# Two conditioning vectors of layer 1: summed along rows by DVE beside the gate projection, in place of matmuls in the attention

## The chip, the cores and the metric

The kernel runs on one core of a Trainium2 chip. The time is device microseconds of one execution of the whole program. Engines: PE (TensorE, matmuls), DVE (VectorE), ACT (ScalarE), POOL (GpSimd) and SP, which here only issues DMAs. Each engine works through its own queue in order; semaphores order them against each other.

## What is computed

One step of a two-layer trunk on 512 latent tokens and 128 context tokens of width 1024. Layer 0 mixes tokens by gated attention, layer 1 by a gated linear recurrence. The change touches only the conditioning: each layer derives a shift, a scale and a gate from two vectors (`c` for latent tokens, `c_ctx` for context tokens).

```python
def _adaln(cond, w, b):
    mod = jax.nn.silu(cond.astype(jnp.float32)) @ w.astype(jnp.float32) + b.astype(jnp.float32)
    mod = mod.astype(cond.dtype)
    return jnp.split(mod, 3, axis=-1)

for i in range(DEPTH):
    sh_p, sc_p, g_p = _adaln(c_ctx, ada_w[i], ada_b[i])
    sh_s, sc_s, g_s = _adaln(c, ada_w[i], ada_b[i])
    hp = xp * (1.0 + sc_p) + sh_p
    hs = xs * (1.0 + sc_s) + sh_s
    ...
```

So per layer there is a product of a 2 x 1024 matrix with a 1024 x 3072 matrix (12 MB of weights). Layer 0's shift and scale are needed before anything else; layer 0's gate at its output projection; layer 1's shift and scale after layer 0; layer 1's gate at the end.

## The kernel before

Tokens lie in five tiles of 128 (`TT`), features in eight (`KT`). Float32 products are made of three matmuls of split operands (high and low part), so each weight piece of 128 x 1024 is loaded (`raw`), cast by ACT to its high part (`whi`, L232) and reduced to its low part by DVE (`wlo`, L233).

The first half of the program (up to the output projection of layer 0) is put in order by a scheduler that works on a simulated timeline; DMAs and some other instructions wrapped in `pin` keep their program order. The stages there are:

- lead-in, to about 55 us: layer 0's shift and scale (`ada_feat`, from `ada_m`), the modulated input `hhi`/`hlo`, keys and values (`acc`);
- query chunk 0 (`pmm`) and then the gate projection (`gps`, 16 steps of 24 matmuls over the weight chunks 6 to 9). In its steps the list `later` splits the queries of chunk 0 (`q_job`: `qn`, `u`, `r`, then `qs`) and the keys (`k_split`, `klo`), and PE turns them (`qps`, `kps`). The norm of the queries takes a power on POOL (`rq`) behind DVE's `rs_t`;
- attention (`att_gen`): scores `sc`, row maximum `nm` on DVE (L936), exponential `p` on ACT (L941), its scaling on POOL (L947), transposes `pt`, products `pot`. Two units of scores run ahead of the products. Beside it a list `side` is woven in at a fixed ratio: the query chunks 1, 2, 3 (`q_gen`, `qmm`), and then the loading and splitting of the output weights.

What the change touches is `ada_gen`. The vectors `ada_s` are four blocks of 1024 x 1024: 0 is layer 0's gate, 1 and 2 are layer 1's shift and scale, 3 is layer 1's gate. Each is eight pieces (`raw`, 512 KB); `ada_mms` (L276) multiplies a piece with the Silu of the vectors, on 32 columns of the array per quarter, and DVE adds the result into `acc` (L327). Block c − 1 runs in the filler of query chunk c, block 3 behind the last of them:

```python
    def q_next(c):
        Xs[c] = xq[c % 2].tile([P, 4, NT], F32R, tag="X", name=f"X{c}")
        yield from q_gen(c, Xs[c], ada_gen((c - 1,)))
    ...
    side.items.append(("a", ada_gen((3,)), lambda: back_of[0] == 3))
```

All weight pieces come through one ring of three buffers (`rawp`) in the order of the list `order`, at most two ahead (`RAW_AHEAD`), issued by SP.

Of the kernel before, what the change touches and what calls it, by code (L numbers as in the profile page):

```python
# [11 lines left out]
F32 = mybir.dt.float32  # L12
# [6 lines left out]
P = 128  # L19
# [28 lines left out]
D_ST = 3.0  # L48
D_OUT = 5.5
SLIP = 1.0  # L50


def view(t, off, dims):
# [78 lines left out]
def hybrid_step(ctx: ExitStack, tc: tile.TileContext, a: dict, o: dict):  # L132
# [62 lines left out]
    def pump():  # L195
        while order:
            start = order[0] in FIRST
            if len(ahead) >= (RAW_START if start else RAW_AHEAD):
                break
            src = order.popleft()  # L200
            if src[0] == "x":
                c = slice(src[1] * CW, (src[1] + 1) * CW)
                pin(nc.sync.dma_start(xt[:, :TS, c], a["xs"][:, c].rearrange("(t p) d -> p t d", p=P)))
                pin(nc.sync.dma_start(xt[:, TS, c], a["xp"][:, c]))
                continue
            if src[0] == "rope":
                rope_loads()
                continue
            raw = (raw0 if start else rawp).tile([P, 1024], F32, tag="raw", name="raw")
            if src[0] == "kvh":  # L210
                pin(nc.sync.dma_start(raw[:, :512], piece(src)))
            else:
                (pass_on if src[0][:3] == "rec" else pin)(nc.sync.dma_start(raw, piece(src)))
            ahead.append((src, raw))

    def piece(src):
        name, c, i = src
        if name == "kvh":
            return a["attn_kv"][0][:, i * 512:(i + 1) * 512]
        if name == "ada_s":  # L220
            return a[name][c][i * P:(i + 1) * P, :]
        return a[name][c][:, i * 1024:(i + 1) * 1024]

    def split_piece(hi, lo, src, lo_eng=None, after=()):
# [75 lines left out]
        nc.vector.tensor_copy(row, ps[:, :CW])  # L300
        return row

    def ada_out(sup, acc):

        if sup % 3 == 0:
            for q in range(4):
                nc.gpsimd.dma_start(gated[sup // 3][:, q * CW:(q + 1) * CW], acc[32 * q:32 * q + 2, :])
            return
        ps = bank1("adaps2")
        for j in range(2):  # L310
            nc.tensor.transpose(ps[:, j * P:(j + 1) * P], acc[:, j * P:(j + 1) * P], ident)
        for j in range(2):
            nc.vector.tensor_scalar(view(shsc[1], (sup - 1) * 2 * KT + 2 * j, [[4, 4], [1, 2]]),
                                    view(ps, j * P, [[32, 4], [1, 2]]), float(sup - 1), 0.0, ALU.add, ALU.add)
# [5 lines left out]
    def ada_gen(sups):  # L320
        for sup in sups:
            acc = rowp.tile([P, CW], F32, tag="row", name="acc")
            nc.gpsimd.dma_start(acc, a["ada_bias"][sup])
            for i in range(4):
                ps = bank1("adaps")
                ada_mms(ps, sup, i)
                nc.vector.tensor_tensor(acc, acc, ps[:, :CW], ALU.add)  # L327
                yield
            yield
            ada_out(sup, acc)  # L330
            yield
            if sup == 0:
                gate_load(0, nc.gpsimd)

    def feat_mms(ps, w, mt, j, hhi, hlo):
        c, t = slice(mt * P, (mt + 1) * P), slice(*HALVES[j])
# [73 lines left out]
    gate[0] = gsp.tile([P, 2, D], F32, tag="gate", name="gate0")  # L410
# [241 lines left out]
    def split_k(r, n, col):  # L652
# [6 lines left out]
        def back():  # L659
            for i in range(n):  # L660
# [9 lines left out]
                nc.scalar.copy(kk[:, :, c], ps.rearrange("p (a b) -> p a b", a=NKV))  # L670
                for e in range(2):
                    r = slice(HD * e, HD * (e + 1))
                    nc.vector.tensor_copy(klo[r, e::2, c], ps2[r, :2 * P].rearrange("p (a b) -> p a b", a=2))
        return back

    last_split = []
# [65 lines left out]
    def lead_in(att):  # L742
# [77 lines left out]
        later += [lambda n=n: k_split(n) for n in range(3)]  # L820
        step = 0
        for ch in range(6, 10):
            if ch < 9:
# [2 lines left out]
            for mt in range(2):  # L826
                for j, (t0, t1) in enumerate(HALVES):
# [5 lines left out]
                        settle()  # L833
                    if step % 2 and later:
                        later.pop(0)()
                    if step > 16 - EARLY:
                        next(att)


    def score_mms(out, X, c, h, t0, k0, k1):  # L840
# [181 lines left out]

    side = Side()
    att = att_gen(side)
    lead_in(att)
    holding[0] = False
    for fn in held:
        pin(fn())
# [668 lines left out]
def _layout(inputs):  # L1697
    g = {k: np.asarray(v) for k, v in inputs.items()}
    r = _constants()
    r["xs"], r["xp"] = g["x_sample"][0], g["x_prompt"][0]  # L1700
    cond = np.stack([g["c"][0], g["c_ctx"]]).reshape(2, KT, P).transpose(2, 1, 0).reshape(P, -1)
# [4 lines left out]
    r["ada_s"] = np.stack([w[0][:, 2 * D:]] + [w[1][:, i * D:(i + 1) * D] for i in range(3)])  # L1706
    rows = np.zeros((4, 4, 32, CW), np.float32)
    rows[:, :, :2] = g["ada_b"].reshape(6, 4, 1, CW)[2:]
    r["ada_bias"] = rows.reshape(4, P, CW)
# [34 lines left out]
```

## Time and profile before

| | |
|---|---|
| median of 3 runs | 845.42 us (845.3 to 845.75) |
| profiled execution | 845.58 us, its span 843.5 us |
| granted TensorE clock, mean | 0.988 |
| PE, DVE, ACT, POOL busy | 816.5, 532.1, 380.3, 213.6 us |
| HBM read, written | 82.06 MB, 9.19 MB |

A row of a timeline has the start in us from the span's start, the duration, the engine, the line, the operation, the tile written, the tiles read and the shapes; in brackets stands how long the engine was idle before it and what ended that. A row of a group has the count, the total busy time and the mean duration in ns. A row of windows has the stretch, and for each engine its busy time and its instructions; `PEclk` is the granted clock as a share of full speed.

### The profile page before, as it was taken

How to read it: one execution, taken by the hardware profiler on the slowest of the kernel's cores; microseconds unless marked ns; L12 is line 12 of the kernel's file. 1: busy time of each engine (PE TensorE's matmuls, PEld its weight loads, DVE VectorE, ACT ScalarE, POOL GpSimd, SP SyncE). 2: the span in 40 equal slices, each digit the busy share in tenths (PEclk: the TensorE clock that was granted, in tenths of full speed). 3: DMA queues.
4: the chain of work that ended last, by engine and by line, in shares of the span. 5: the costliest groups of instructions: out<-in, count | busy, mean ns of one | idle time of the engine just before them, and what ended most of it. 6: DMA issues, size and time to landing. Idle time of an engine off the chain costs nothing.

```text
span 843.5 us, 19410 instructions
## 1 busy us (share of the span) xinstructions
PE 816.5 (97%) x8157; PEld 732.1 (87%) x8157; DVE 532.1 (63%) x954; ACT 380.3 (45%) x769; POOL 213.6 (25%) x263
## 2 busy tenths in 40 slices
PE   8999999989999998999999999999999999999994
PEld 6789999768888766888999999999999999998774
DVE  3675534665557666776438575767668575858476
ACT  2242535563556767222434534435434544445232
POOL 0123001535334743010001304143333314121121
PEclk8999999999999999999999999999999999999997
DMA  9923120145141245630323322331332323314041
GB/s 330 387 86 105 55 72 26 52 162 196 51 157 52 100 133 169 225 125 35 111 66 67 108 68 82 83 108 52 107 89 83 93 67 89 120 65 157 26 157 75
DMA packets 34134, 92.50 MB, mean 110 GB/s; under 512 B 5040, under 2 KB 12224, under 8 KB 34048
## 3 DMA queue, kind: packets, MB, share of 16 engines
q1 hardware_dynamic: 23280, 73.05, 25.9%
q0 software_dynamic: 4864, 14.44, 5.7%
q10 hardware_dynamic: 5904, 3.78, 1.5%
q8 instruction: 64, 1.05, 0.5%
q14 instruction: 22, 0.18, 0.1%
HBM read 82.06 MB, written 9.19 MB: 108 GB/s over the span
## 4 chain that ended last, share of the span: by engine, by line
PE 89%; DVE 5%; ACT 2%; DMA 2%; issue 1%; POOL 1%; SPq 0%; DVEq 0%; ACTq 0%; POOLq 0%
PE rps L1289 7%; PE rps L1290 7%; PE rps L1291 7%; PE vgps L1279 5%; PE vgps L1280 5%; PE vgps L1281 5%; PE pot L868 4%; PE outp L1128 4%; PE pt L954 4%; PE outp L1130 3%; PE outp L1129 3%; PE acc L525 3%; PE lv L1422 2%; PE gps L338 2%; PE gps L340 2%; PE gps L339 2%
## 5 line engine op out<-in xcount | busy, mean ns | idle before, releaser
L1289 PE MATMUL rps<-h1hi,rhi 128*128 128x320 f32 x368 | 118.3, 321 | 0.0
L1290 PE MATMUL rps<-h1lo,rhi 128*128 128x320 f32 x368 | 113.8, 309 | 0.0
L1291 PE MATMUL rps<-h1hi,rlo 128*128 128x320 f32 x368 | 113.6, 309 | 0.0
L947 POOL TENSOR_SCALAR p<-p,rc 128x640 f32<-128x640 f32 x64 | 56.0, 878 | 124.0 <-DVE rc L946 112.7
L1289 PEld LDWEIGHTS rps<-h1hi,rhi 128*128 128x128 f32 x368 | 69.1, 188 | 1.3
L1290 PEld LDWEIGHTS rps<-h1lo,rhi 128*128 128x128 f32 x368 | 69.2, 188 | 0.0
L1291 PEld LDWEIGHTS rps<-h1hi,rlo 128*128 128x128 f32 x368 | 69.1, 188 | 0.0
L233 DVE TENSOR_TENSOR rlo<-raw,rhi 128x1024 fp32r<-128x1024 f32 x32 | 45.1, 1411 | 33.9 <-ACT rhi L232 33.9
L941 ACT ACTIVATE p<-sc,nm 128x640 f32<-128x640 f32 x64 | 51.4, 804 | 31.0 <-DVE nm L936 18.6
L936 DVE TENSOR_REDUCE nm<-sc 128x1 f32<-128x640 f32 x64 | 52.0, 818 | 21.2 <-PE sc L842 21.1
L1450 POOL COPY At<-near 32x160 f32<-32x160 f32 x32 | 14.0, 438 | 195.2 <-DVE near L1412 194.2
L232 ACT CAST rhi<-raw 128x1024 fp32r<-128x1024 f32 x32 | 33.6, 1049 | 51.8 <-PE rps L1290 48.7
L1400 ACT COPY kc<-A 128x640 f32<-128x640 f32 x40 | 32.2, 806 | 54.0 <-DVE A L1431 50.1
L1279 PE MATMUL vgps<-rhi,h1hi 128*128 128x256 f32 x180 | 51.5, 286 | 0.0
L1280 PE MATMUL vgps<-rlo,h1hi 128*128 128x256 f32 x180 | 50.9, 283 | 0.0
L1281 PE MATMUL vgps<-rhi,h1lo 128*128 128x256 f32 x180 | 50.8, 282 | 0.0
L954 PE MATMUL pt<-small,p 128*128 128x128 f32 x320 | 49.6, 279 | 0.8 <-ACT pts L846 0.5
L841 PE MATMUL sc<-kk,X 128*128 128x320 f32 x128 | 42.9, 344 | 5.0 <-ACT p L941 5.0
L954 PEld LDWEIGHTS pt<-small,p 128*128 128x128 f32 x320 | 36.8, 141 | 10.1 <-issue 5.6
L846 ACT COPY pts<-pt 128x512 f32<-128x512 f32 x64 | 36.8, 594 | 17.4 <-PE pt L954 17.3
L1279 PE MATMUL vgps<-wspare,h1hi 128*128 128x256 f32 x140 | 41.7, 298 | 0.0
L338 PE MATMUL gps<-hhi,whi 128*128 128x320 f32 x128 | 40.0, 313 | 0.4 <-ACT X L693 0.4
(298 smaller groups left out, 2393.7 us busy)
## 6 DMA issues: line engine op xcount, KB each, us to landing
raw<-in_rec_w_in SPq DMA_DIRECT2D x40, 512.0 KB, 3.7
raw<-in_ada_s SPq DMA_DIRECT2D x32, 512.0 KB, 4.3
raw<-in_ada_m SPq DMA_DIRECT2D x16, 512.0 KB, 7.9
raw<-in_attn_w_in SPq DMA_DIRECT2D x16, 512.0 KB, 4.6
raw<-in_attn_w_out SPq DMA_DIRECT2D x8, 512.0 KB, 4.3
raw<-in_rec_w_out SPq DMA_DIRECT2D x8, 512.0 KB, 3.9
x1d<-y SPq DMA_DIRECT2D x5, 512.0 KB, 2.6
rx<-x1d POOLq DMA_DIRECT2D x20, 128.0 KB, 3.2
```

The costliest lines, as they stand in the source:

```text
L233: (lo_eng or nc.gpsimd).tensor_tensor(lo, raw, hi.bitcast(F32), ALU.subtract)
L338: nc.tensor.matmul(ps[:, :320], w.hi(k)[:, c], hhi[:, k, t], start=(k == 0), stop=False)
L936: nc.vector.tensor_reduce(nm[:, 0:1], sc[:, :, :320], AX.XY, ALU.max, negate=True)
L941: return nc.scalar.activation(halves(p[:]), sc[:, :, :320], AF.Exp, bias=nm[:, 0:1], accum_out=su[:, 0:1])
L947: nc.gpsimd.tensor_scalar(p, p, rs[:, 0:1], 1.0, ALU.mult, ALU.mult)
L954: nc.tensor.transpose(pt[:, i * 256 + q * P:i * 256 + (q + 1) * P], ps[q][:, (k0 + i) * P:(k0 + i + 1) * P], ident)
L1279: nc.tensor.matmul(out, h1hi[:, k, t], hi, start=(k == 0), stop=False)
L1280: nc.tensor.matmul(out, h1hi[:, k, t], lo, start=False, stop=False)
L1281: nc.tensor.matmul(out, h1lo[:, k, t], hi, start=False, stop=(k == KT - 1))
L1289: nc.tensor.matmul(ps[:, j, :320], hi[:, k, :], h1hi[:, k, t], start=(k == 0), stop=False)
L1290: nc.tensor.matmul(ps[:, j, :320], hi[:, k, :], h1lo[:, k, t], start=False, stop=False)
L1291: nc.tensor.matmul(ps[:, j, :320], lo[:, k, :], h1hi[:, k, t], start=False, stop=(k == KT - 1))
```

## The change

Layer 1's shift and scale no longer go through PE. Their weights are given transposed (`ada_c`: 16 pieces, one per vector and feature tile, with the output feature on the partition), and the Silu of both vectors is loaded in every partition (`silb`, 128 x 2 x 1024). For each piece DVE multiplies it with one vector and sums along the row into one column of `shsc[1]`, twice (once per vector): 32 operations of 128 x 1024 with a summed output. The product itself is written to scratch: 12 pieces use the part of `gs` that holds its last two tiles, the last four use a tile of `prep`.

Twelve pieces are worked off in steps 1 to 12 of the gate projection, through two extra buffers (`adar`) with their own loads; four (`COLS_LATE`) in the filler of query chunk 1, through the common ring. Block 0 moves to the filler of query chunk 2, block 3 to that of query chunk 3, and the list entry behind them goes. The Silu of `silb` is made by ACT in the lead-in; `silb` uses the buffer of layer 0's gate, whose load comes behind block 0 as before. The `klo` casts of the keys (12 of them) go from DVE to ACT.

```diff
+COLS = [(s, ft) for s in range(2) for ft in range(KT)]
+COLS_LATE = 4
...
+            if src[0] == "sil":
+                for s in range(2):
+                    pin(nc.sync.dma_start(silb[:, s, :], a["cond_r"][s:s + 1, :].to_broadcast((P, D))))
+                continue
...
-    def ada_out(sup, acc):
-
-        if sup % 3 == 0:
-            for q in range(4):
-                nc.gpsimd.dma_start(gated[sup // 3][:, q * CW:(q + 1) * CW], acc[32 * q:32 * q + 2, :])
-            return
-        ps = bank1("adaps2")
-        for j in range(2):
-            nc.tensor.transpose(ps[:, j * P:(j + 1) * P], acc[:, j * P:(j + 1) * P], ident)
...
+    def ada_cols(job, raw, spill):
+
+        s, ft = job
+        for c in range(2):
+            nc.vector.scalar_tensor_tensor(spill, raw, 1.0, silb[:, c, :], ALU.mult, ALU.mult,
+                                           accum_out=shsc[1][:, s, ft, c:c + 1])
+        if ft == KT - 1:
+            nc.vector.tensor_tensor(shsc[1][:, s], shsc[1][:, s], view(adab, (3 + s) * KT, [[1, KT], [0, 2]]), ALU.add)
+
+    def cols_gen():
+        for job in COLS[len(COLS) - COLS_LATE:]:
+            ada_cols(job, take(("ada_c",) + job), prep.tile([P, D], F32, tag="s2", name="spill", bufs=2))
+            pump()
             yield
...
+    order.append(("sil",))
     FIRST = set(order)
...
     for c in range(3):
         order.extend(pieces("attn_w_in", c + 1))
-        order.extend(ada_pieces(c))
-    order.extend(ada_pieces(3))
+        order.extend(ada_pieces(c - 1) if c else [("ada_c",) + job for job in COLS[len(COLS) - COLS_LATE:]])
...
-                    nc.vector.tensor_copy(klo[r, e::2, c], ps2[r, :2 * P].rearrange("p (a b) -> p a b", a=2))
+                    nc.scalar.copy(klo[r, e::2, c], ps2[r, :2 * P].rearrange("p (a b) -> p a b", a=2))
...
+            if n == 1:
+                nc.scalar.activation(silb, silb, AF.Silu)
...
+        def cols_load():
+            if cols:
+                raw = adar.tile([P, D], F32, tag="raw", name="adaraw")
+                pin(nc.sync.dma_start(raw, piece(("ada_c",) + cols[0])))
+                raws.append((cols.popleft(), raw))
+
+        for _ in range(2):
+            cols_load()
...
                     if step % 2 and later:
                         later.pop(0)()
+                    if raws:
+                        ada_cols(*raws.popleft(), gs[:, KT - 2:, :].rearrange("p a b -> p (a b)")[:, :D])
+                        cols_load()
...
-        yield from q_gen(c, Xs[c], ada_gen((c - 1,)))
+        yield from q_gen(c, Xs[c], ada_gen(c - 2) if c > 1 else cols_gen())
...
-    side.items.append(("a", ada_gen((3,)), lambda: back_of[0] == 3))
```

The scheduler places the new operations. First, DVE's queue in the first gate steps, from the statistic of the queries (`rs_t`) to the split of their first tiles (`qs`). Before:

```order
L188 TENSOR_SCALAR rs_t<-ssq 128x20
L604 TENSOR_TENSOR qn<-pmm,rq 128x512
L643 TENSOR_TENSOR u<-qn,sinq 128x512
L645 TENSOR_TENSOR r<-qn,cosq 128x512
L647 TENSOR_TENSOR r<-r,u 128x512
L683 TENSOR_TENSOR qs_914<-r,qs_914 128x8x64
```

The same place now (`adaraw` is a piece of the transposed weights, `gs` the scratch, `shsc` the sum):

```order
L190 TENSOR_SCALAR rs_t<-ssq 128x20
L335 SCALAR_TENSOR_TENSOR gs,shsc_80<-adaraw,silb 128x1024 x3
L615 TENSOR_TENSOR qn<-pmm,rq 128x512
L335 SCALAR_TENSOR_TENSOR gs,shsc_80<-adaraw,silb 128x1024
L654 TENSOR_TENSOR u<-qn,sinq 128x512
L656 TENSOR_TENSOR r<-qn,cosq 128x512
L335 SCALAR_TENSOR_TENSOR gs,shsc_80<-adaraw,silb 128x1024
L658 TENSOR_TENSOR r<-r,u 128x512
L615 TENSOR_TENSOR qn<-pmm,rq 128x512
L335 SCALAR_TENSOR_TENSOR gs,shsc_80<-adaraw,silb 128x1024
L654 TENSOR_TENSOR u<-qn,sinq 128x512
L694 TENSOR_TENSOR qs_924<-r,qs_924 128x8x64
```

Six summed operations and two operations of the next tiles (`qn`, `u`) now stand between `rs_t` and `qs`; two more summed operations stand a little ahead of `rs_t`. On PE the transposes of `qs` still stand behind the first 96 gate matmuls, as before.

Second, DVE's queue at the end of the gate projection, where the first row maxima (`nm`) of the attention stand. Before:

```order
L936 TENSOR_REDUCE nm<-sc 128x1
L233 TENSOR_TENSOR wlo<-raw,whi 128x1024
L936 TENSOR_REDUCE nm<-sc 128x1
L946 RECIPROCAL rc<-su 128x1 x2
L936 TENSOR_REDUCE nm<-sc 128x1 x2
L946 RECIPROCAL rc<-su 128x1
```

And now (`raw` is a late piece, `spill` the scratch in `prep`):

```order
L964 TENSOR_REDUCE nm<-sc 128x1
L241 TENSOR_TENSOR wlo<-raw,whi 128x1024
L964 TENSOR_REDUCE nm<-sc 128x1
L974 RECIPROCAL rc<-su 128x1 x2
L335 SCALAR_TENSOR_TENSOR spill,shsc_80<-raw,silb 128x1024
L964 TENSOR_REDUCE nm<-sc 128x1
L335 SCALAR_TENSOR_TENSOR spill,shsc_80<-raw,silb 128x1024
L964 TENSOR_REDUCE nm<-sc 128x1
L974 RECIPROCAL rc<-su 128x1
```

A summed operation now stands ahead of the third and of the fourth row maximum; six more follow between the maxima while query chunk 1 is made.

Third, SP's queue from the first attention weights to the output weights. Before:

```order
L213 DMA raw<-in_attn_w_in 128x1024 x12
L213 DMA raw<-in_ada_s 128x1024 x8
L213 DMA raw<-in_attn_w_in 128x1024 x2
L213 DMA raw<-in_ada_s 128x1024 x8
L213 DMA raw<-in_attn_w_in 128x1024 x2
L213 DMA raw<-in_ada_s 128x1024 x16
L213 DMA raw<-in_attn_w_out 128x1024 x8
```

And now:

```order
L213 DMA silb<-in_cond_r 128x1024 x2
L219 DMA raw<-in_attn_w_in 128x1024 x6
L840 DMA adaraw<-in_ada_c 128x1024 x2
L219 DMA raw<-in_attn_w_in 128x1024 x2
L840 DMA adaraw<-in_ada_c 128x1024 x4
...
L219 DMA raw<-in_ada_c 128x1024 x4
L219 DMA raw<-in_attn_w_in 128x1024 x2
L219 DMA raw<-in_ada_s 128x1024 x8
L219 DMA raw<-in_attn_w_in 128x1024 x2
L219 DMA raw<-in_ada_s 128x1024 x8
L219 DMA raw<-in_attn_w_out 128x1024 x8
```

The loads of the transposed pieces stand between the weights of the gate projection, each behind the operation on DVE that frees its buffer; the weights of query chunk 2 stand behind four transposed pieces where eight pieces for PE stood.

More of the change, by code (lines that the diff above doesn't have):

```diff
@@ L221, in piece @@
             return a[name][c][i * P:(i + 1) * P, :]
+        if name == "ada_c":
+            return a[name][c, i]
         return a[name][c][:, i * 1024:(i + 1) * 1024]
@@ L318, in gate_load, with ada_gen @@
             eng.dma_start(gate[layer][:, s, :], gated[layer][s:s + 1, :].to_broadcast((P, D)))
[L320 to L328, printed above, removed]
-            yield
-            ada_out(sup, acc)
+    def ada_gen(layer):
+        acc = rowp.tile([P, CW], F32, tag="row", name="acc")
+        nc.gpsimd.dma_start(acc, a["ada_bias"][layer])
+        for i in range(4):
+            ps = bank1("adaps")
+            ada_mms(ps, layer, i)
+            nc.vector.tensor_tensor(acc, acc, ps[:, :CW], ALU.add)
+            yield
+        yield
+        for q in range(4):
+            nc.gpsimd.dma_start(gated[layer][:, q * CW:(q + 1) * CW], acc[32 * q:32 * q + 2, :])
+        yield
+        if layer == 0:
+            gate[0] = gsp.tile([P, 2, D], F32, tag="gate", name="gate0")
+            gate_load(0, nc.gpsimd)
+    def ada_cols(job, raw, spill):
[9 more added lines that the diff above has]
+            pump()
             yield
-            if sup == 0:
-                gate_load(0, nc.gpsimd)
     def feat_mms(ps, w, mt, j, hhi, hlo):
@@ L409, in hybrid_step @@
     xt = gsp.tile([P, TT, D], F32, tag="gs", name="xt")
-    gate[0] = gsp.tile([P, 2, D], F32, tag="gate", name="gate0")
+    silb = gsp.tile([P, 2, D], F32, tag="gate", name="silb")
     qtab = rpool("qtab", 1)
@@ L820, in lead_in @@
         later += [lambda n=n: k_split(n) for n in range(3)]
+        cols = deque(COLS[:len(COLS) - COLS_LATE])
+        raws = deque()
+        def cols_load():
[5 more added lines that the diff above has]
+            cols_load()
         step = 0
@@ L835, in lead_in @@
                         later.pop(0)()
+                    if raws:
+                        ada_cols(*raws.popleft(), gs[:, KT - 2:, :].rearrange("p a b -> p (a b)")[:, :D])
+                        cols_load()
                     if step > 16 - EARLY:
                         next(att)
+        assert not raws
     def score_mms(out, X, c, h, t0, k0, k1):
@@ L1024, in hybrid_step @@
     att = att_gen(side)
+    adar_st = ExitStack()
+    adar = adar_st.enter_context(pool("adar", 2, side="right"))
     lead_in(att)
+    adar_st.close()
     holding[0] = False
@@ L1700, in _layout @@
     r["xs"], r["xp"] = g["x_sample"][0], g["x_prompt"][0]
-    cond = np.stack([g["c"][0], g["c_ctx"]]).reshape(2, KT, P).transpose(2, 1, 0).reshape(P, -1)
+    r["cond_r"] = np.stack([g["c"][0], g["c_ctx"]])
+    cond = r["cond_r"].reshape(2, KT, P).transpose(2, 1, 0).reshape(P, -1)
     ada_b = g["ada_b"].reshape(2, 3, KT, P).transpose(3, 0, 1, 2).reshape(P, -1)
@@ L1705, in _layout @@
     w = g["ada_w"]
[L1706 to L1709, printed above, removed]
+    r["ada_s"] = np.stack([w[i][:, 2 * D:] for i in range(2)])
+    r["ada_c"] = w[1][:, :2 * D].T.reshape(2, KT, P, D)
+    rows = np.zeros((2, 4, 32, CW), np.float32)
+    rows[:, :, :2] = g["ada_b"].reshape(2, 3, 4, 1, CW)[:, 2]
+    r["ada_bias"] = rows.reshape(2, P, CW)
     r["attn_w_in"], r["attn_w_out"] = _chunks(g["attn_w_in"][0]), _chunks(g["attn_w_out"][0], 512)
```

3 lines of the change are left out of this document (removed).

## The prediction

> **What bounds the kernel now.** I read the page's busy times and its chain first. The chain is the work that ended last, followed backwards, in shares of the span.
>
> ```profile
> PE 816.5 (97%) x8157; PEld 732.1 (87%) x8157; DVE 532.1 (63%) x954; ACT 380.3 (45%) x769; POOL 213.6 (25%) x263
> ...
> PE 89%; DVE 5%; ACT 2%; DMA 2%; issue 1%; POOL 1%; SPq 0%; DVEq 0%; ACTq 0%; POOLq 0%
> ```
>
> PE carries 89% of the chain, so work taken off PE can pay and work put on DVE is free only while DVE is not waited for. That is a matter of the stage, so I asked for the busy time of each engine by stretch: chunk 0 of the queries and the first gate matmuls (72 to 89), the rest of the gate projection (89 to 131), the attention while query chunk 1 is made (147 to 186), a disturbed stretch (186 to 194), and the attention's end (300 to 337).
>
> ```profile
> core 0: us, PE busy (x) PEld busy (x) DVE busy (x) ACT busy (x) POOL busy (x), PEclk, DMA share, GB/s
> 72.00:89.00 17.00, 16.61 (x119) 16.46 (x118) 10.27 (x16) 5.70 (x11) 3.57 (x1) 1.00 0.20 63
> 89.00:131.00 42.00, 42.00 (x307) 41.96 (x306) 15.31 (x25) 17.27 (x30) 0.00 (x0) 1.00 0.20 64
> ...
> 147.00:186.00 39.00, 38.20 (x334) 29.99 (x332) 25.90 (x61) 22.48 (x53) 17.34 (x17) 1.00 0.27 96
> 186.00:194.00 8.00, 5.94 (x39) 4.44 (x42) 4.87 (x8) 4.18 (x9) 5.79 (x8) 0.79 0.73 221
> ...
> 300.00:318.00 18.00, 17.52 (x164) 11.31 (x161) 10.64 (x27) 10.74 (x29) 8.26 (x11) 1.00 0.56 185
> 318.00:337.00 19.00, 16.82 (x135) 12.24 (x133) 12.80 (x24) 14.20 (x27) 7.39 (x10) 1.00 0.50 159
> ```
>
> PE is full everywhere but in 186 to 194 and 318 to 337. DVE has 26.7 us free in 89 to 131, but only 6.7 in 72 to 89.
>
> **The change: what leaves PE.** The conditioning matmuls of the attention are one group; one piece of the chain shows 16 in a row.
>
> ```profile
> L276 PE MATMUL adaps<-raw,sil 128*32 128x256 f32 x256 | 18.8, 395 | 0.9 <-DMA raw<-in_ada_s 0.7 <-ACT p L941 0.2
> 168.05 1.00 PE adaps L276 x16
> ```
>
> Sixteen take 1.00 us of PE, so the 256 take 16.0 and the half that goes 8.0: a quarter (4.0) from the stretch of query chunk 1 and a quarter from the attention's end. (The two middle quarters stay in number; the four transposes that go too are left at nothing.) At the end, where PE is busy 17.52 of 18, I count all 4.0. In 147 to 186 DVE gets eight new operations, some 10 us beside its 25.90 of 39; I count 3.0 of the 4.0. Together −7.0.
>
> **What comes on DVE, and its price.** No operation with a summed output runs on DVE before, so I bound it. The rows: the same operation on 512 columns without a sum, a two-input operation on 1024 columns, and the instruction that reads ACT's accumulator.
>
> ```profile
> L1145 DVE SCALAR_TENSOR_TENSOR y<-x,y 128x512 f32<-128x512 f32 x10 | 6.9, 691 | 0.3
> L233 DVE TENSOR_TENSOR wlo<-raw,whi 128x1024 fp32r<-128x1024 f32 x8 | 9.8, 1224 | 6.0 <-ACT whi L232 6.0
> L941 ACT ACTIVATION_READ_ACCUMULATOR p<-sc,nm 128x1 f32 x64 | 13.1, 205 | 0.0
> ```
>
> From 512 to 1024 columns adds 0.533 us, which puts the new operation at 1.22 us. With a readout like ACT's it is at most 1.43. In a queue 1024 columns cost 1.14 (72.72 to 73.86 below). So 1.14 to 1.43 each; I take 1.25, nearest the row with its shape. 32 of them are 40 us, 24 in the gate projection. [...]
>
> **The first query transposes.** Here DVE is the one waited for. DVE's timeline, then PE's:
>
> ```profile
> 71.65 0.68 DVE L643 TENSOR_TENSOR u<-kr,sink 128x512 f32<-128x512 f32 x1
> 72.72 1.22 DVE L233 TENSOR_TENSOR wlo<-raw,whi 128x1024 fp32r<-128x1024 f32 x1 [0.39 <-ACT whi L232]
> 73.86 0.68 DVE L645 TENSOR_TENSOR kr<-kr,cosk 128x512 f32<-128x512 f32 x1
> ...
> 76.53 0.17 DVE L188 TENSOR_SCALAR rs_t<-ssq 128x20 f32<-128x20 f32 x1
> 80.39 0.69 DVE L604 TENSOR_TENSOR qn<-pmm,rq 128x512 f32<-128x512 f32 x1 [3.69 <-POOL rq L189]
> ...
> 84.59 0.69 DVE L683 TENSOR_TENSOR qs<-r,qs 128x512 fp32r<-128x512 f32 x1 [1.45 <-ACT qs L682]
> 86.93 0.80 PE L691 MATMUL qps<-identr,qs 128*128 128x128 f32 x8
> 88.12 0.41 PE L338 MATMUL gps<-hhi,whi 128*128 128x320 f32 x1 [0.39 <-ACT X L693]
> ```
>
> PE reaches the transposes at 86.93; their input qs is ready at 85.28. In the new order eight summed operations stand ahead of qs. Two are ahead of rs_t: 2.5, less the idle 0.39, so rs_t ends about 2.1 later, and POOL's answer, 3.69 behind it, comes at 82.5. Three (3.75) fit into that wait. Behind qn stand three more (3.75) and six operations (before: four between qn and qs take 4.20 − 1.45, or 0.69 each; six are 4.1). So qs starts at 82.5 + 3.75 + 4.1 = 90.35 and ends at 91.0: PE waits 4.1 us. With 1.14 each and a shorter pitch of 0.61 it is 3.2; with 1.43 it is 5.3. Everything behind in PE's queue, the remaining gate matmuls, waits too.
>
> A wait of this size also costs clock. The one disturbed stretch of the attention shows it; SP's, ACT's and PE's rows, and a short window:
>
> ```profile
> 180.40 2.34 SPq L213 DMA_DIRECT2D raw<-in_attn_w_in  x2
> 185.07 1.05 ACT L232 CAST whi<-raw 128x1024 fp32r<-128x1024 f32 x1 [3.81 <-DMA raw<-in_attn_w_in]
> 187.93 0.41 PE L841 MATMUL sc<-kk,X 128*128 128x320 f32 x1 [1.66 <-ACT p L941]
> 189.18 1.08 PE L276 MATMUL adaps<-raw,sil 128*32 128x256 f32 x8 [0.40 <-DMA raw<-in_ada_s]
> 190.00:192.00 2.00, 2.00 (x13) 1.81 (x10) 1.32 (x2) 0.59 (x1) 1.97 (x3) 0.50 0.61 166
> ```
>
> PE idled 2.06 us in 186 to 194 and then ran at a granted clock of 0.50; over those 8 us the clock was 0.79, a loss of 0.21 × 8 = 1.7. I add 1.7 to the wait of 4.1: +5.8 (3.2 without the clock, 7.0 at the most). [...]
>
> Later DVE catches up: to 131 it has 20.5 us of its old work left (10.27 + 15.31, less 5.1 for the casts that leave) and 30 new in 59, and the next query splits are wanted only after PE's own delay. Should loads land late, SP waits on DVE there, and DVE on SP: the two buffers need one load of 4.3 per two operations of 2.5 each.
>
> ```profile
> raw<-in_ada_s SPq DMA_DIRECT2D x32, 512.0 KB, 4.3
> L673 DVE CAST klo<-kps 64x256 fp32r<-64x256 f32 x12 | 5.1, 422 | 13.8 <-PE kps L668 13.7
> ```
>
> Those casts go to ACT, busy 17.27 of 42 in 89 to 131: nothing, and at most the 5.1 if ACT were full.
>
> **The disturbed stretch.** It costs 2.06 + 1.7 = 3.8 now. Its cause: ACT's cast of the chunk-2 weights waited 3.81 us for a load that SP could issue only at 180.40, when PE had used the conditioning pieces in the three raw buffers, and the exponentials stand behind that cast. In the new order these buffers are emptied by DVE, and the chunk-2 loads come earlier; but then the first conditioning piece of chunk 2 waits for the last summed operation and its own 4.3, which I put at 2.0 of PE's time. Gain 1.7, from 0 to 3.8.
>
> **The start of the attention.** Two summed operations stand ahead of row maxima that DVE is asked for at once:
>
> ```profile
> 139.65 0.82 DVE L936 TENSOR_REDUCE nm<-sc 128x1 f32<-128x640 f32 x1 [0.55 <-PE sc L842]
> 141.07 0.82 DVE L936 TENSOR_REDUCE nm<-sc 128x1 f32<-128x640 f32 x1 [0.60 <-PE sc L842]
> ```
>
> The idle 0.55 and 0.60 in front take 1.15 of their 2.5; I count half of the rest, +0.6 (0 to 1.4).
>
> **In the lead-in** ACT gets one Silu over 2048 columns. Its neighbours there, and two rows for its length:
>
> ```profile
> 45.68 1.05 ACT L232 CAST kvhi<-raw 128x1024 fp32r<-128x1024 f32 x1
> 48.99 0.73 ACT L481 CAST hhi<-h 128x640 fp32r<-128x640 f32 x1 [2.26 <-DVE h L474]
> L830 ACT ACTIVATE gs<-gps 128x320 f32<-128x320 f32 x16 | 7.0, 437 | 32.9 <-PE gps L340 32.9
> L1311 ACT ACTIVATE s<-rps 128x640 f32<-128x640 f32 x24 | 16.8, 701 | 0.2
> ```
>
> 320 more columns cost 0.264, so 2048 cost about 1.9, in a gap of 2.26: nothing; uncovered it would be 1.9. Its two loads go on SP behind the last conditioning weights; late by 4.3 they would cost the same 1.9.
>
> **The sum**, against the profiled execution's 845.58 (span 843.5 and 2.1 around it): −7.0 + 5.8 − 1.7 + 0.6 = −2.3, so 843.3. The median of the runs is 0.16 lower: 843.1. A measurement of this kernel can tell about 0.2%, 1.7 us, from no change.
>
> **Rivals.** (1) *The first transposes are not late.* For it: three of the eight operations lie in POOL's wait. Against: the other five lie on the path by the order itself. Without wait and clock loss 843.1 − 5.8 = 837.3; with the wait alone 841.4. Chance 0.14. (2) *DVE holds up the softmax* in the stretch of query chunk 1, and the kernel is slower. Each of the eight summed operations there takes 1.25 ahead of a row maximum, in an in-order queue. For it: DVE has 13.1 of 39 us free for 10. Against: two score blocks run ahead. All on the path cost 10.0 where I counted 0.6: 852.5; half of it 847.8. It decides against the change from about a third on. Chance 0.26. [...] Chance 0.12. (4) *The matmuls that go had filled waits* for ACT and DVE, as 318 to 337 with PE busy 16.82 of 19 suggests for the end: 4 of the 7.0 are not realised, 847, no measurable change or just slower. Chance 0.10.
>
> **The numbers.** My case has 0.38, from 840.5 to 845.5: 0.28 faster, 0.10 the same. Faster 0.28 + 0.14 = 0.42. The same 0.10, 0.02 of rival 2 and 0.05 of rival 4: 0.17. Slower 0.24 + 0.12 + 0.05 = 0.41. From 838 to 853 leaves out rival 3, some 0.04 of rival 1 and 0.02 of rival 2. Both signs hold much of it, so the likeliest case's own range is 840.5 to 845.5.
>
> **What would show it.** Right: summed operations of about 1.25 us; PE idle about 4 us ahead of the first query transposes, near 87, with a granted clock near 0.5 behind it; none after that up to 131; the attention some 6 to 7 us shorter. Wrong: summed operations over 2 us; no idle PE at 87; PE waiting for row maxima in 150 to 190; or an attention as long as before.

## The result, and the profile after

The changed kernel takes 844.14 us (median of 14 runs, 841.21 to 846.96); before takes 844.85 in the runs beside it (14 runs, 841.89 to 846.02). The ratio is 0.9996, with a 95% interval of 0.9982 to 1.0011: no change that can be measured, where the forecast was 0.27% faster. The forecast change lies just outside the interval, which ends at 0.18% faster. The profiled execution has 844.78 us and a span of 843.0.

The page's busy times and chain, as they are after the change:

```profile
PE 808.0 (96%) x8025; PEld 729.2 (87%) x8025; DVE 559.9 (66%) x996; ACT 386.5 (46%) x782; POOL 215.8 (26%) x261
...
PE 82%; DVE 9%; ACT 2%; DMA 2%; issue 2%; POOL 1%; SPq 0%; DVEq 0%; ACTq 0%; POOLq 0%
```

PE lost 8.5 us of work and the span 0.5. On the chain PE's share fell by 7 points and DVE's rose by 4: what left PE came back as time in which PE waits. To see where, I cut both executions at the first and the last gate matmul (gps) and at the first output matmul (outp). The windows of before, then of after (columns: span, then busy time and count of PE, PEld, DVE, ACT, POOL, PE's granted clock, DMA share, GB/s):

```profile
72.86:135.46 62.60, 62.21 (x448) 62.02 (x447) 26.73 (x42) 23.77 (x41) 3.57 (x1) 1.00 0.19 60
135.46:337.00 201.54, 193.83 (x1637) 154.63 (x1636) 127.54 (x287) 125.07 (x280) 89.39 (x95) 0.99 0.34 115
```

```profile
72.17:140.78 68.61, 64.46 (x448) 64.00 (x447) 48.65 (x79) 27.99 (x53) 4.47 (x1) 0.95 0.40 131
140.78:336.82 196.04, 183.49 (x1504) 150.49 (x1503) 133.98 (x292) 125.13 (x280) 90.67 (x93) 1.00 0.25 84
```

The gate projection grew by 6.0 us and the attention shrank by 5.5. The rest of the difference is the lead-in (72.17 for 72.86) and 0.3 behind the attention. In the attention PE is busy 10.3 us less, but idle 12.55 instead of 7.71.

The gate projection first: the timeline of DVE ahead of the first query transposes and of PE at them, and then the clock in short windows behind.

```profile
82.45 0.69 DVE L615 TENSOR_TENSOR qn<-pmm,rq 128x512 f32<-128x512 f32 x1 [0.85 <-POOL rq L191]
83.06 1.21 DVE L335 SCALAR_TENSOR_TENSOR gs<-adaraw,silb 128x1024 f32<-128x1024 f32 x1
...
85.40 1.22 DVE L335 SCALAR_TENSOR_TENSOR gs<-adaraw,silb 128x1024 f32<-128x1024 f32 x1
...
87.75 1.22 DVE L335 SCALAR_TENSOR_TENSOR gs<-adaraw,silb 128x1024 f32<-128x1024 f32 x1
...
89.49 0.69 DVE L694 TENSOR_TENSOR qs<-r,qs 128x512 fp32r<-128x512 f32 x1
90.33 1.23 PE L702 MATMUL qps<-identr,qs 128*128 128x128 f32 x8 [3.92 <-DVE qs L694]
```

```profile
88.00:90.00 2.00, 0.00 (x0) 0.00 (x0) 2.00 (x4) 0.00 (x0) 0.00 (x0) 0.69 0.03 10
90.00:92.00 2.00, 1.45 (x9) 1.29 (x10) 2.00 (x5) 0.86 (x2) 0.00 (x0) 0.50 0.99 348
92.00:94.00 2.00, 2.00 (x8) 2.00 (x9) 2.00 (x4) 0.50 (x2) 0.00 (x0) 0.50 0.41 166
94.00:96.00 2.00, 2.00 (x11) 2.00 (x10) 2.00 (x4) 1.21 (x2) 0.00 (x0) 0.61 0.02 4
```

Three summed operations stand between qn and qs. Counted from the first gate matmul, qs ends at 18.0 us where it ended at 12.4 (90.18 − 72.17 and 85.28 − 72.86). PE waits 3.92, the clock falls in the course of that wait, at 88.7, and stays at 0.50 up to 95.6. PE's busy time in the stage, 64.46 for 62.21, shows the clock's price: 2.2. POOL's part changed too: its one operation in the stage, the power that gives rq, took 4.47 us beside three summed operations, where it took 3.57 before.

The stretches that the prediction read, where they moved, and the two groups of summed operations (gate projection, attention):

```profile
72.00:89.00 17.00, 14.40 (x99) 14.14 (x98) 16.01 (x28) 3.69 (x7) 4.47 (x1) 0.99 0.40 124
89.00:131.00 42.00, 40.45 (x281) 40.26 (x282) 31.24 (x50) 21.27 (x40) 0.00 (x0) 0.92 0.49 164
...
300.00:318.00 18.00, 15.61 (x120) 11.73 (x122) 11.03 (x25) 12.79 (x32) 8.15 (x9) 1.00 0.24 79
318.00:337.00 19.00, 16.83 (x127) 12.10 (x124) 9.68 (x24) 11.79 (x25) 7.05 (x9) 1.00 0.00 1
```

```profile
L335 DVE SCALAR_TENSOR_TENSOR gs<-adaraw,silb 128x1024 f32<-128x1024 f32 x24 | 29.3, 1223 | 3.5 <-DMA adaraw<-in_ada_c 3.1
L335 DVE SCALAR_TENSOR_TENSOR spill<-raw,silb 128x1024 f32<-128x1024 f32 x8 | 10.5, 1312 | 0.0
```

In 300 to 318 PE, which was full with 17.52 of 18, now has 15.61: the filler has gone and no other work came up. That row is the one to pursue.

### The profile page after: what moved, and what is told of

The parts are those of the page before. It is cut to its first block, busy times and chain, and to the rows that moved or that the text cites. A ratio compares the mean times of both kernels' runs of the same rounds, so it can differ in the third digit from the quotient of the medians.

```text
span 843.0 us, 19206 instructions
## 1 busy us (share of the span) xinstructions
PE 808.0 (96%) x8025; PEld 729.2 (87%) x8025; DVE 559.9 (66%) x996; ACT 386.5 (46%) x782; POOL 215.8 (26%) x261
## 4 chain that ended last, share of the span: by engine, by line
PE 82%; DVE 9%; ACT 2%; DMA 2%; issue 2%; POOL 1%; SPq 0%; DVEq 0%; ACTq 0%; POOLq 0%
PE rps L1319 7%; PE rps L1320 7%; PE rps L1321 7%; PE vgps L1309 5%; PE vgps L1311 5%; PE vgps L1310 5%; PE pot L896 4%; PE outp L1158 4%; PE outp L1160 3%; PE outp L1159 3%; PE pt L982 3%; PE lv L1452 2%; PE acc L536 2%; PE gps L349 2%; PE sc L869 2%
## 5 line engine op out<-in xcount | busy, mean ns | idle before, releaser
L975 POOL TENSOR_SCALAR p<-p,rc 128x640 f32<-128x640 f32 x64 | 58.8, 921 | 116.6 <-DVE rc L974 102.3
L1320 PEld LDWEIGHTS rps<-h1lo,rhi 128*128 128x128 f32 x368 | 69.3, 188 | 0.0
L896 PE MATMUL pot<-pts,vv 128*64 128x256 f32 x320 | 38.9, 386 | 2.4 <-DVE pts L874 2.4
```

Of the source, the lines that this page charges most:

```text
L896: nc.tensor.matmul(pot[j * HD:(j + 1) * HD, :CW], vv[:, slot, c * HD:(c + 1) * HD], moving[j], start=first, stop=last)
L975: nc.gpsimd.tensor_scalar(p, p, rs[:, 0:1], 1.0, ALU.mult, ALU.mult)
L1320: nc.tensor.matmul(ps[:, j, :320], hi[:, k, :], h1lo[:, k, t], start=False, stop=False)
```

## The experiments

Theory A at the start: two costs on DVE eat the gain, the late qs in the gate projection and the eight late summed operations in the attention. Rivals: C, the gate projection is longer because of twelve more loads or a full DVE; B, the matmuls that left PE had only filled waits. For every kernel below I give the three cuts, read as above from its rows for gps and outp. "Clock lost" is two-microsecond windows times (1 − clock) within the attention; "waits behind 245" adds up PE's waits from 245 us to the first outp matmul.

| kernel | median us | ratio to before (95%) | lead-in | gate projection | attention | clock lost there | waits behind 245 |
|---|---|---|---|---|---|---|---|
| before | 843.6 to 844.9 | 1 | 72.9 | 62.6 | 201.5 | 1.7 | 3.2 |
| changed | 844.14 | 0.9996 (0.9982 to 1.0011) | 72.2 | 68.6 | 196.0 | 0 | 7.2 |
| e1, after qs | 841.08 | 0.9970 (0.9953 to 0.9988) | 70.7 | 63.8 | 199.0 | 3.4 | 7.4 |
| e2, gate ones narrow | 839.97 | 0.9949 (0.9929 to 0.9968) | 70.9 | 64.3 | 196.0 | 0 | 7.1 |
| e3, late ones narrow | 843.10 | 0.9995 (0.9983 to 1.0008) | 71.3 | 69.3 | 193.7 | 0 | 7.1 |
| e4, all narrow | 838.13 | 0.9936 (0.9913 to 0.9959) | 72.7 | 63.3 | 193.9 | 0 | 7.2 |
| e5, block to the end | 842.74 | 0.9995 (0.9973 to 1.0017) | 73.4 | 63.8 | 196.4 | 0 | 7.2 |
| e6, before, end block out | 846.05 | 1.0031 (1.0013 to 1.0048) | 71.4 | 62.6 | 204.8 | 5.1 | 6.9 |
| e7, before, first block out | 835.37 | 0.9912 (0.9889 to 0.9935) | 69.9 | 62.6 | 194.4 | 0 | 3.2 |
| e8, two late | 844.32 | 1.0018 (0.9997 to 1.0039) | 71.0 | 65.3 | 199.0 | 3.4 | 6.7 |
| e9, half moved | 836.71 | 0.9930 (0.9903 to 0.9957) | 71.5 | 65.3 | 193.1 | 0 | 3.2 |
| e10, klo on DVE | 843.39 | 1.0012 (0.9994 to 1.0030) | 71.0 | 68.7 | 195.6 | 0 | 6.8 |

The lead-in differs by up to 3.5 us between executions, and by 2.7 between two kernels that are the same up to there (e1 and e5), so single times are compared by the later cuts.

### e1: the summed operations held behind qs

```
-                    if raws:
-                        ada_cols(*raws.popleft(), ...)
+                    if raws and step >= 1:
+                        with ExitStack() as hold:
+                            for ins in last_split:
+                                hold.enter_context(tc.issue_after(ins))
+                            ada_cols(*raws.popleft(), ...)
```

> All 32 summed operations and all loads stay; the 24 of the gate projection may only issue once the latest rotated and split query part (qs) has, so that none stands between the query statistics and the first qs. Theory A (the changed kernel loses its gain first to the late qs: PE waits 3.9 us before the first query transposes and runs at half clock behind): gate projection from first to last gps matmul about 62.5 us instead of 68.6, no PE wait of over 0.5 us before the first transposes, clock 1.00, time about 838 (844.1 - 6). Rival C (the stage is longer because of the twelve 0.5 MB loads or of a DVE that is simply too full): stage still 66 us or more, the idle time only moved to later transposes or to wlo, time 842 to 844.

The gate projection's window, and the timeline's rows for qs and for the transposes:

```profile
70.70:134.50 63.80, 62.40 (x448) 62.05 (x447) 49.87 (x79) 28.05 (x53) 3.57 (x1) 1.00 0.42 141
```

```profile
82.43 0.70 DVE L694 TENSOR_TENSOR qs<-r,qs 128x512 fp32r<-128x512 f32 x1 [1.45 <-ACT qs L693]
83.04 1.22 DVE L335 SCALAR_TENSOR_TENSOR gs<-adaraw,silb 128x1024 f32<-128x1024 f32 x1
85.96 0.54 PE L702 MATMUL qps<-identr,qs 128*128 128x128 f32 x4 [0.73 <-ACT X L704]
```

All 24 operations and their loads are there, DVE is as busy as in the changed kernel (49.87 for 48.65), and 4.8 of the 6.0 us are back. So it is their place in the queue, not their number, nor the loads: C falls. The remaining 1.2 is mostly two waits of PE for ACT's copies of the transposes. The time did not fall by 6. It is 0.30% (2.5 us) below before's runs beside it, where the changed kernel was 0.04% below its own: about 2.2 us gained, and the two intervals still touch. In the profiled execution the attention is 199.0 instead of 196.0, because PE's clock fell at 294 (the last section shows it).

### e2, e3 and e4: summed operations of 32 columns

```
-            nc.vector.scalar_tensor_tensor(spill, raw, 1.0, silb[:, c, :], ...)
+            nc.vector.scalar_tensor_tensor(spill[:, :w], raw[:, :w], 1.0, silb[:, c, :w], ...)
```

The width w is 32 for the 24 of the gate projection (e2), for the eight late ones (e3), or for all (e4).

> The 24 summed operations of the gate projection read 32 columns instead of 1024 (so layer 1's shift and half of its scale are sums over a part only); loads, their buffers and the order of issue stay. Each should cost about 0.2 us instead of 1.22. Theory A: stage 62.5 us, time about 838, as with the operations held behind qs; the attention stays at 196. Rival C in its form with the loads: stage 66 us or more, time 842 to 844.

> The eight summed operations in the stretch of query chunk 1 (attention) read 32 columns instead of 1024 (the other half of layer 1's scale is a sum over a part only); all else stays. Theory A (they stand ahead of row maxima and hold ring buffers, which makes PE idle 12.5 us in the attention instead of 7.7): gate projection stays at 68.6, attention 196.0 falls to 191 to 192, the PE waits for p and pts fall back to before's 5.0 and 0.5 us, time about 839.5. Rival B (the matmuls taken off PE had filled waits that come back whatever DVE does): attention stays at 195 to 196, time 843 to 844.

> All 32 summed operations read 32 columns (layer 1's shift and scale are sums over a part only): the removal from PE without the cost on DVE. Theory A: the full 8.0 us of the matmuls and about 3.8 of the disturbed stretch show, gate projection 62.5, attention 190 to 192, time 833 to 835. Rival B (filled waits): attention 195 to 196, time about 838. If the two costs add, the difference to the changed kernel is the sum of the differences of the two kernels with one of them narrowed.

The attention's window of e3, and both windows of e4:

```profile
140.58:334.27 193.69, 183.19 (x1506) 150.54 (x1504) 127.27 (x292) 124.89 (x280) 87.58 (x93) 1.00 0.25 85
```

```profile
72.67:135.98 63.31, 62.42 (x448) 62.01 (x447) 25.15 (x77) 27.81 (x53) 3.57 (x1) 1.00 0.42 142
135.98:329.87 193.89, 183.29 (x1505) 150.48 (x1504) 127.26 (x292) 124.98 (x280) 87.53 (x93) 1.00 0.26 85
```

In the stages the two costs add: 4.3 us in the gate projection (e2, which keeps a wait of 1.57 ahead of the transposes; 5.3 in e4) and 2.2 in the attention (196.0 to 193.7 and 193.9). The late operations cost half of what Theory A put on them. The 2.2 rest on the profiled executions alone: e3's ratio of 0.9995 is the changed kernel's 0.9996, though its mean clock over the runs is also lower (0.989 for 0.992). PE's waits near them, in the changed kernel and then in e3:

```profile
182.97 0.41 PE L869 MATMUL sc<-kk,X 128*128 128x320 f32 x1 [0.85 <-ACT p L969]
184.48 2.38 PE L896 MATMUL pot<-pts,vv 128*64 128x256 f32 x20 [0.66 <-DVE pts L874]
190.11 0.64 PE L284 MATMUL adaps<-raw,sil 128*32 128x256 f32 x8 [1.15 <-DMA raw<-in_ada_s]
```

```profile
182.49 0.42 PE L869 MATMUL sc<-kk,X 128*128 128x320 f32 x1 [0.36 <-ACT p L969]
```

2.3 us of waits here are what the late operations cost: 1.15 of pts and of the softmax, 1.15 of a load that could start only when the last of them had emptied its buffer. But with nothing left on DVE, e4 is still idle for 10.6 us in its attention, against before's 7.7, and only 5.4 us (0.64%) faster than before where 8.0 of matmuls and 3.8 of the disturbed stretch had gone. Theory A does not cover this. What is left lies behind 245: 7.1 to 7.2 us of waits in all four kernels, 3.2 in before. In the changed kernel:

```profile
291.84 0.33 PE L702 MATMUL qps<-identr,qs 128*128 128x128 f32 x2 [1.02 <-DVE qs L694]
296.43 1.38 PE L982 MATMUL pt<-small,p 128*128 128x128 f32 x8 [0.59 <-ACT pts L874]
298.55 0.41 PE L869 MATMUL sc<-kk,X 128*128 128x320 f32 x1 [0.74 <-ACT p L969]
301.63 0.41 PE L869 MATMUL sc<-kk,X 128*128 128x320 f32 x1 [1.71 <-ACT p L969]
```

This gave Theory A2: rival B holds for the attention's end, and there alone. Before's timeline shows its fourth block at work in that place, from the first piece to the last:

```profile
304.36 1.07 PE L276 MATMUL adaps<-raw,sil 128*32 128x256 f32 x16
...
317.22 0.64 PE L276 MATMUL adaps<-raw,sil 128*32 128x256 f32 x8 [0.29 <-DMA raw<-in_ada_s]
```

### e6 and e7: before, with one block of matmuls left out

```
-                ada_mms(ps, sup, i)
-                nc.vector.tensor_tensor(acc, acc, ps[:, :CW], ALU.add)
+                if sup == 3:                                # e7: sup == 0
+                    for k in (2 * i, 2 * i + 1):
+                        take(("ada_s", sup, k))
+                        pump()
+                else:
+                    ada_mms(ps, sup, i)
+                    nc.vector.tensor_tensor(acc, acc, ps[:, :CW], ALU.add)
```

> The kernel before with its fourth block of 64 conditioning matmuls (and the four additions behind them) left out at the attention's end; its loads stay (gate 1 is the bias alone). Theory A2: nothing to speak of is gained, attention 201 to 202 us, ratio 0.999 to 1.001, and the waits for p and qs that the changed kernel shows near 291 to 302 appear. Rival D, and the prediction's own reading (PE is full there, so all 4.0 us count): attention 197 to 198, ratio 0.995.

> The kernel before with its first block of 64 conditioning matmuls (and the four additions behind them) left out in the stretch of query chunk 1; its loads stay (gate 0 is the bias alone). Theory A2: the 4.0 us of matmuls count in full there, and with them goes the disturbed stretch at 186 to 194 (3.8 us of waits and half clock, on loads of this block and behind them) at least in part: attention 194 to 197.5, ratio 0.991 to 0.995. Rival (waits there too): attention 200 or more, ratio 0.998 or more.

Two of PE's waits in e6, and e7's attention:

```profile
299.38 0.41 PE L846 MATMUL sc<-kk,X 128*128 128x320 f32 x1 [2.00 <-ACT p L946]
...
310.55 1.95 PE L873 MATMUL pot<-pts,vv 128*64 128x256 f32 x16 [1.37 <-DVE pts L851]
```

```profile
132.52:326.96 194.44, 187.59 (x1574) 152.26 (x1572) 125.41 (x283) 124.72 (x280) 84.18 (x88) 1.00 0.33 113
```

This settles it. Without its end block the kernel before is not faster but slower, by 0.31% (0.13 to 0.48), which is more than A2 allowed: the waits grow from 3.2 to 6.9, and in the profiled execution the clock falls once more at one of them, at about 300 to 303, and for longer, to 0.50, at 187 to 194. Over all runs the mean clock is 0.990 for before's 0.992. With the clock's loss taken off, its attention is as long as before's: 204.8 − 5.1 = 199.7, and 201.5 − 1.7 = 199.8. Four microseconds of PE work there are worth nothing. The first block alone, left out in query chunk 1, is worth 0.88% (0.65 to 1.11), some 7.4 us: in its attention PE is busy 6.2 us less (4.0 of matmuls and before's 1.7 of clock, which leaves 0.5 without a cause) and idle 0.9 less.

### e5 and e8: the remaining block moved into the end

```
-        yield from q_gen(c, Xs[c], ada_gen(c - 2) if c > 1 else cols_gen())
+        yield from q_gen(c, Xs[c], (cols_gen(), ada_gen(0), empty_gen())[c - 1])
...
+    side.items.append(("a", ada_gen(1), lambda: back_of[0] == 3))
```

Both also hold the gate projection's operations behind qs; e8 has 28 of them and four late. `empty_gen` only yields: query chunk 3 gets no conditioning work.

> On top of the kernel whose summed operations follow qs (841.1): gate 1's block of 64 conditioning matmuls (4.0 us of PE) goes from the stretch of query chunk 3, where PE is full, to the attention's end, where the kernel before has its fourth block. Theory A2 (the matmuls taken from the attention's end only filled waits there: from the value products at 280 to the first outp matmul it took 56.6 us before and 57.2 us after, 4.0 us of matmuls fewer): the waits of 1.0, 0.6, 0.7 and 1.7 us near 291 to 302 go, the attention falls by about 4, time about 837 (ratio to before about 0.992). Rival D (the end is longer for another reason, for instance the casts and row maxima of the last chunk): the attention stays as long, time 841.

> As the kernel with the block moved to the end, and two of the four late pairs of summed operations moved from query chunk 1 into the gate projection (28 there, 4 late). If the late ones cost 2.2 us for eight (attention 196.0 with them, 193.8 with 32 columns each) because each stands ahead of a row maximum, half of it goes: attention 1.1 us shorter and time about 836. If DVE is too full at the end of the gate projection (it was busy 49 of 64 us there with 24), the first row maxima of the attention are late instead and it is no faster, or slower by 1 to 3.

e5 missed, with 842.74 us for about 837. The end has its filler again, but the stretch of chunk 3 has lost it, and PE's waits behind 245 are again 7.2 us, only in other places, among them these:

```profile
282.84 0.54 PE L702 MATMUL qps<-identr,qs 128*128 128x128 f32 x4 [0.80 <-DVE qs L694]
...
313.47 0.41 PE L872 MATMUL sc<-kk,X 128*128 128x320 f32 x1 [1.37 <-ACT p L972]
```

So A2 was drawn too narrowly: query chunk 3 and the end are one stretch, in which PE waits for the softmax's steps (p, pts, qs) and two blocks of filler fit into these waits; whichever is taken out comes back as waits of 4 us (e9 below keeps both, and has 3.2). What in the softmax sets that pace these runs do not tell apart (in the changed kernel ACT has 12.79 and DVE 11.03 of 18 in 300 to 318, and neither is full). e8 missed its 836 too, and says little more: the waits at 179 to 187 shrank from 2.5 us in e5 to 0.4, those at the attention's start grew from 1.7 to 2.6, and its clock fell three times (88, 146 and 330), for 3.4 us in the attention.

### e9: half the change

Only layer 1's scale goes to DVE (16 summed operations, all behind qs); the shift stays on PE in chunk 3, gate 1 at the end, and chunk 1 has no conditioning at all.

```
-COLS = [(s, ft) for s in range(2) for ft in range(KT)]
-COLS_LATE = 4
+COLS = [(1, ft) for ft in range(KT)]
+COLS_LATE = 0
...
+        yield from q_gen(c, Xs[c], (empty_gen(), ada_gen(0), ada_gen(2))[c - 1])
...
+    side.items.append(("a", ada_gen(1), lambda: back_of[0] == 3))
```

> Only layer 1's scale goes to DVE: 16 summed operations, all in the gate projection and each held behind the latest qs, none in the attention. The shift stays on PE (64 matmuls and two transposes, in query chunk 3), gate 0 in chunk 2, and gate 1 at the attention's end, so that query chunk 1 has no conditioning matmul and the end keeps its filler. Theory A3 (a block taken from chunk 1 is worth 7.1 us of attention, a second one taken from the end nothing; 24 operations behind qs cost the gate projection 1.2 us): gate projection 63 to 64, attention 194 to 195, nothing lost to late operations in chunk 1; time about 836 to 837, ratio to before 0.991 to 0.993, faster than the changed kernel by about 0.8%. Rival (the second block counts too, so that half the change keeps half the gain and the lost time is only late operations): attention 197 or more, time 840 or more.

Its two windows, and PE's waits in the gate projection:

```profile
71.50:136.82 65.32, 63.91 (x448) 63.58 (x447) 40.35 (x63) 27.70 (x53) 3.57 (x1) 0.97 0.33 106
136.82:329.88 193.06, 186.68 (x1571) 152.10 (x1570) 125.37 (x281) 124.64 (x280) 87.47 (x94) 1.00 0.29 97
```

```profile
86.76 0.54 PE L712 MATMUL qps<-identr,qs 128*128 128x128 f32 x4 [0.73 <-ACT X L714]
87.98 0.41 PE L358 MATMUL gps<-hhi,whi 128*128 128x320 f32 x1 [0.68 <-ACT X L714]
```

836.71 us, ratio 0.9930 (0.9903 to 0.9957): faster than both kernels, with half of the work moved; the gate projection came out 1.3 us longer than expected and the attention 0.9 shorter. PE has 3.2 us more to do in the attention than in the changed kernel, and the attention is 3.0 us shorter. In this execution the gate projection lost 1.5 us more than e1's to half clock at the two short waits; the same pair cost clock in e8 and none in e1 and e5 (the last section has the rows).

### e10: the casts of klo back on DVE

```
-                    nc.scalar.copy(klo[r, e::2, c], ps2[r, :2 * P]...)
+                    nc.vector.tensor_copy(klo[r, e::2, c], ps2[r, :2 * P]...)
```

> The changed kernel with the casts of the keys' low parts (klo) back on DVE, as before the change; all else stays. If the casts are free on ACT and DVE's queue behind the first qs has slack (no PE wait between the first transposes and 131), nothing changes: ratio to before 0.9990 to 1.0005. If DVE is the bound of the gate projection (busy 49 of 68.6 us, 31 of 42 in 89 to 131), the casts on it make later transposes or the first row maxima late: gate projection or attention 1 to 2 us longer, ratio 1.001 or more.

Gate projection 68.7 and attention 195.6, about as in the changed kernel, and no wait in the gate projection but the first one and, as there, 0.22 right behind it:

```profile
89.49 1.23 PE L702 MATMUL qps<-identr,qs 128*128 128x128 f32 x8 [4.23 <-DVE qs L694]
```

Its ratio, 1.0012, lies on the side of the second case, but the interval, 0.9994 to 1.0030, holds both cases and overlaps that of the changed kernel. By the stages this part of the change moves nothing that can be told.

## Why the prediction was right and wrong

**The price of a summed operation** (1.25, from 1.14 to 1.43): 1.223 us, 1.14 from its start to that of another operation in DVE's queue, with a readout of 0.08. The eight late ones took 1.31 on the mean. The 0.41 for slower holds 0.12 for the third rival, a longer summed operation that no run shows; in its place the changed kernel showed 1.21 to 1.23 us for the 24 of the gate projection and 1.21 to 1.75 for the eight late ones.

**The first query transposes** (+5.8): 3.92 of wait where 4.1 was worked out and 2.2 of clock where 1.7 was, +6.0 in the stage. e1 shows that it is the order alone. The cause and the place stood, and with them the first rival fell: it would have been right had the operations been put behind qs. That the size stood is in part luck, for two errors met. POOL's answer was taken over as 3.69 behind rs_t and came 4.60 behind it: the power took 4.47 us in the three kernels that have three full summed operations beside it (changed, e3, e10), 3.95 in e7, which has three operations on 512 columns there, and 3.57 in the eight others, where DVE is idle or its operations have 32 columns. And from qn to the end of qs DVE took 7.7 us, not 8.5. The clock's 1.7 came from a fall of 3.4 us; this one lasted 6.8.

**The matmuls that leave PE** (−7.0): this step failed. "At the end, where PE is busy 17.52 of 18, I count all 4.0" measured zero (e6). PE was full in that window because the block filled the softmax's waits, and a full window does not tell filler from need. The fourth rival named this mechanism and got only 0.10. The other side of the term held: in chunk 1 the block counted its 4.0 in full (e7), and the 1.0 taken off for DVE's late operations measured 1.15 in waits for the softmax (e3). The four transposes left at nothing were 0.38 and 0.44 us a pair by their rows.

**The disturbed stretch** (−1.7 of 3.8): the idle time did not go: 0.85, 0.66 and 1.15 stand at 183 to 190 where there were 1.66 and 0.40, the last on the load that was foreseen to be late. Half clock did go, 1.7, in this execution. That part was luck as much as cause: e1's clock fell at 294 behind a wait that the other kernels passed at full clock.

**The start of the attention** (+0.6): PE waits there 0.72, 0.31 and 0.66, where there were 0.94 and 0.20: +0.55. The size was right and the reason wrong. With the operations narrow (e4) the waits are 0.92, 0.31 and 0.65, and with none in e7 1.09, 0.31 and 0.65: the block's matmuls had filled these too, and the summed operations have no part in it.

**DVE and the softmax in chunk 1** (second rival): the eight late operations cost 2.2 us of their 10, a fifth, and half of that was the late load. The rival needed a third to turn the change into a loss.

**The lead-in and the casts** were free as said: ACT's Silu took 1.92 of the gap and left 0.44 of it, and e10 shows the casts at nothing. The loads of the transposed pieces did come late for DVE, 3.1 us in all, but PE waited for none of them. (The two operations of a piece are 2.5 us together, not each, as the text on the two buffers has it.)

Together: −0.7 lead-in, +6.0, −5.5 in the attention where −8.1 was summed, −0.3 behind. The missing 2.6 is the end's 4.0, less 0.8 of transposes that had not been counted and 0.6 in small parts. That the time, 844.14, lies between 840.5 and 845.5 says little for the forecast: the kernel before lies there too, at 844.85 in the runs beside it.

## What to carry to other kernels

A window in which the engine is full does not say that its work there is worth its time: ask what it would do without it, and look at the stretch before and behind for waits on the same chain. Here filler taken from such a stretch was worth nothing (e6), and the same filler taken from a stretch where PE had work queued was worth all of it and the stalls that hung on it (e7), so move the half that pays (e9) and leave the other. And when work is added to an in-order queue, put it behind the item that the bound engine waits for: the order alone was worth 4.8 us of the gate projection here (e1).

## What the runs showed of the hardware

PE's granted clock falls to 0.50 at some waits and not at others of the same length, in code that is the same there. At 1.63 to 1.74 us at the attention's end it stayed at 1.00 in the changed kernel, e2, e3 and e4, and fell for 6.8 us in e1, at 1.72. Behind two waits of 0.73 and 0.67 or 0.68 in 2 us it fell to 0.50 in e9's and e8's gate projection and stayed at 1.00 in e1's and e5's.

In three traces the changes of the clock lie on a grid in time. In before it is at 0.50 from 8.04 to 14.87 and from 188.94 to 192.36, in the changed kernel from 10.24 to 13.65 and from 88.74 to 95.57: 188.94 − 8.04 is 53 steps of 3.413 us and 88.74 − 10.24 is 23, and the falls last one step or two. In e8 the clock falls at 88.04, 146.07 and 330.39 and is back one step later, at 91.45, 149.48 and 333.80: 146.07 − 88.04 is 17 steps of 3.413 us and 330.39 − 146.07 is 54. So I put the windows on these steps. First the two short waits, in e9, where they lie in one step, and in e1, where a step ends between them:

```profile
85.60:89.01 3.41, 2.00 (x16) 1.72 (x15) 3.34 (x7) 1.52 (x3) 0.00 (x0) 1.00 0.45 151
```

```profile
83.05:86.46 3.41, 2.68 (x21) 2.43 (x20) 3.34 (x6) 0.93 (x2) 0.00 (x0) 1.00 0.00 0
86.46:89.88 3.42, 2.75 (x19) 2.71 (x19) 3.35 (x7) 1.38 (x2) 0.00 (x0) 1.00 0.69 219
```

In e9 PE is idle for 1.41 us of one step, and the clock falls with the next step; in e1 it is idle 0.73 and 0.67 in two steps, and the clock stays. It is the same with the long wait at the attention's end, in e1 (the step before the fall and the one behind it) and in the changed kernel:

```profile
291.26:294.67 3.41, 1.65 (x11) 1.07 (x9) 3.41 (x6) 3.11 (x7) 0.27 (x1) 1.00 0.77 252
294.67:298.08 3.41, 2.70 (x12) 2.33 (x12) 2.79 (x6) 2.02 (x5) 1.57 (x3) 0.50 0.70 225
```

```profile
296.96:300.37 3.41, 2.22 (x15) 1.64 (x15) 3.41 (x5) 3.12 (x6) 0.00 (x0) 1.00 0.79 238
300.37:303.78 3.41, 2.15 (x18) 1.75 (x20) 3.26 (x8) 2.92 (x7) 1.57 (x2) 1.00 0.67 220
```

One step of e1 has 1.76 us idle; in the changed kernel the same waits fall into two steps, with 1.19 and 1.26. A fall of 6.8 us costs 3.4 us by the table's measure, and e1's attention came out 3.0 longer. Idle time in a step is not all of it: e2 has a step with 1.59 there and no fall, its clock in the attention being 1.00. Where the steps lie against the program differs from execution to execution (in e9 the step above starts 1.16 us ahead of the first transposes at 86.76, in e1 2.91 ahead of those at 85.96), so I take it as a matter of chance whether such a wait costs clock.

Executions of one kernel spread by 3 to 10 us here, and in the changed kernel and in each of e1 to e10 the longer executions are on the whole those with the lower mean clock (correlation from −0.57 to −0.96). A lead-in that differs by 3.5 may be part of the rest.
